# One pool of buffers for rounded and float tiles, and a fourth operand buffer for weights, in a two-layer fp32 trunk

## The chip, the cores and the metric

The kernel runs on one core of a Trainium2 chip. The metric is the device time of one execution in microseconds; the lower the better. The core's engines are PE (matrix multiplication; its weight loads are told apart as PEld), DVE (vector), ACT (scalar activations), POOL (general, also called GpSimd) and SP (which here only issues DMA transfers). Each engine works through its own queue of instructions in order, and they wait for each other by semaphores. Data lie in SBUF (128 partitions, about 204 KB of each taken here, which is all that is free); PE writes to eight PSUM tiles of 128 x 512 floats.

## The reference

What is computed is a trunk of two residual layers on x, 1024 tokens of width 1024, with 256 memory tokens, all in float32:

```python
for layer in range(2):
    h = rms_norm(x, norm_mix[layer])
    if layer == 0:      # gated linear recurrence: conv of width 4, two sigmoid gates,
                        # an associative scan over the tokens, a gelu gate
        y_mix, xq = rglru_group(h, w_in_a, ...)
    else:               # 8-head causal attention with a forget gate
        y_mix, xq = fox_group(h, w_in_b, ...)
    y_mem = memory_group(xq, mem, ...)            # 4-head cross-attention into 256 tokens
    x = x + concatenate([y_mix, y_mem], -1) @ w_out[layer]
    x = x + square(relu(rms_norm(x, norm_mlp[layer]) @ w_mlp_in[layer])) @ w_mlp_out[layer]
```

## The kernel before, in words

**Products.** Each float32 operand is split into a rounded high part ("hi", type fp32r) and the rounded rest ("lo"), and a product is the sum of three matrix products: hi x hi, hi x lo, lo x hi (`t3`). So every activation tile needs two rounded buffers, and every weight a high and a low one. `split` and `split_sb` do it for activations: ACT writes hi, DVE subtracts and writes lo. PE accumulates into a PSUM tile, and DVE or ACT reads it out ("evicts" it).

**Buffers.** Activations live in two sets made once at the start: 60 rounded buffers `r` (128 x 512, fp32r) and 23 float buffers `f` (128 x 515, float32; the three more columns are for the convolution's overlap of tokens). `Slots.get` takes the buffer that was given back longest ago, `Slots.put` gives one back. A piece of code that takes a buffer can start when the last reader of the earlier content is done.

**Weights.** `self.plan` lists all weights in the order of use. An SP load brings one into one of two raw buffers `wr` (L241), ACT rounds it into `wh` (L245), DVE or POOL subtracts into `wl` (L246). `wh` and `wl` have three entries each, used in turn; `wnext` hands out entry i after it has issued the split of entry i + 2. Which of a weight's quarters go to POOL is given by `self.pool_parts`, which the program sets anew at each stage and `_wsplit` reads when it issues the split.

**The order.** The program is written with Python generators: a main stage is woven with a side stage at given rates (`weave`). On top of that the framework's scheduler simulates the written program and sets each engine's order by it, so that a buffer that comes free earlier changes the order on several engines.

**Stages.** The tokens are two halves of 512. In the profiled execution, from the span's start: 0 to 150 us the input projections, the memory's keys and values and the first half's recurrence; 150 to 255 us cross-attention (`xattn`) and the second half's projections; 255 to 330 us the first output projection of the first half (`outproj`), with the second half's recurrence (`lru_scan`, `lru_out`) woven in, and that of the second half (`outproj2`); 330 to 1000 us the first MLP; 1000 to 1600 us the attention layer; 1600 to 2206 us the second MLP. An MLP has 8 groups of hidden columns; its second product is done in 4 blocks a group, each with 7 products in place of 8 (a fast matrix product), whose results are added into x tiles that are loaded from and stored to DRAM (`xspill`) for each block.

**Lines that the steps touch.** In `outproj`, each of eight slices is loaded into a float buffer (`load_x`, L400), PE's product is added to it (L790, `f <- f, pspj`) and it is stored (L794). `lru_scan` works on four column blocks in two passes: L744 to L746 on DVE make the scan's factors, then L756, L757 and L758 on DVE: multiply, rescale, scan; `lru_out` multiplies by the gate (L770), and a split follows (L365/L366 or L371/L372: hi on ACT, lo on DVE). L609 is the cross-attention's product with the values, which the split of L371/L372 evicts from PSUM tile `pso`. PSUM tiles are named after their use: `pspj`, `pss`, `pspt`, `pso`. The MLP's products are L923, its first projection and all other projections are issued by L301 (`mmq`).

Of the kernel before, what the change touches and what calls it, by code (L numbers as in the profile page):

```python
# [10 lines left out]
F32 = mybir.dt.float32  # L11
F32R = mybir.dt.float32r
# [7 lines left out]
P = 128  # L20
S = 1024
D = 1024
H = 512
# [27 lines left out]


class Slots:
    def __init__(self, tiles):
        self.free_ = deque(tiles)
        self.low = len(tiles)

    def get(self):
        t = self.free_.popleft()
        self.low = min(self.low, len(self.free_))  # L60
        return t

    def put(self, *ts):
        for t in ts:
            self.free_.append(t)


def drain(g):
# [69 lines left out]


class Builder:  # L140
    NR = 60
    NF = 23
    FW = 515
    PB = {"pj": 2, "s": 2, "pt": 3, "o": 1}

    def __init__(self, ctx, tc, ins, out):
        self.tc, self.nc, self.ins, self.out = tc, tc.nc, ins, out
        nc = self.nc
        cst = ctx.enter_context(tc.tile_pool(name="cst", bufs=1))
        self.sm = ctx.enter_context(tc.tile_pool(name="sm", bufs=2))  # L150
        self.ps = ctx.enter_context(tc.tile_pool(name="ps", bufs=1, space=PSUM))
        self.dr = ctx.enter_context(tc.tile_pool(name="dr", bufs=1, space=DRAM))
        self.cst = cst

        self.R = Slots([cst.tile([P, 512], F32R, name=f"r{i}") for i in range(self.NR)])
        self.F = Slots([cst.tile([P, self.FW], F32, name=f"f{i}") for i in range(self.NF)])
        self.wraw = [cst.tile([P, 1056], F32, name=f"wr{i}") for i in range(2)]
        self.whi = [cst.tile([P, 1056], F32R, name=f"wh{i}") for i in range(3)]
        self.wlo = [cst.tile([P, 1056], F32R, name=f"wl{i}") for i in range(3)]

        self.par = cst.tile([P, NPAR], F32, name="par")
        nc.sync.dma_start(self.par, ins["par"])
        self.ident = cst.tile([P, P], F32, name="ident")
        make_identity(nc, self.ident)
        self.ones = cst.tile([P, P], F32, name="ones")
        nc.vector.memset(self.ones, 1.0)
        self.cD = cst.tile([P, 1], F32, name="cD")
        nc.vector.memset(self.cD, 1.0 / D)
        self.grp = None
        self.grp_prev, self.grp_cur = [], []  # L170
        self.plan = []
        self.ridx, self.nraw = [], 0
        self.wpos = self.wload = self.wrawn = 0
        self.rs_tok = [None, None]
        self.vx = [None, None]
        self.rsb = [None, None]
        self.ss = [None, None]
        self.uid = 0
        self.pool_parts = TUNE["pa"]
        self.done = set()  # L180
        self.zz = {}
        self.xg = [None, None]
        self.ymix = [None, None]
        self.hs = [None, None]
        self.ymem = [None, None]
        self.xqs = [None, None]
# [93 lines left out]
    def wnext(self):  # L280
        i = self.wpos
        self.wpos += 1
        self._wsplit(i + 3)
        return self._wbuf(i, self.whi), self._wbuf(i, self.wlo)

    def wpair(self):
        i = self.wpos
        self.wpos += 2
        self._wsplit(i + 3)
        return [(self._wbuf(j, self.whi), self._wbuf(j, self.wlo)) for j in (i, i + 1)]  # L290


# [391 lines left out]

    def lru_u(self, h, m, ps):
        nc = self.nc
        u = self.F.get()
        nc.vector.tensor_tensor(u[:, 3:515], ps, self.rsb[h][:, :H], ALU.mult)
        nc.vector.tensor_copy(u[:, 0:3], self.halo[m])
        if h == 0:  # L690
            nc.vector.tensor_copy(self.halo[m], u[:, 512:515])
        uc = self.F.get()
        c = uc[:, :H]
        nc.vector.tensor_scalar(c, u[:, 0:512], self.pc("conv", m), self.pc("convb", m), ALU.mult, ALU.add)
        for j in range(1, 4):
            nc.vector.scalar_tensor_tensor(c, u[:, j:j + 512], self.pc("conv", j * 4 + m), c, ALU.mult, ALU.add)
        self.F.put(u)
        return uc

    def lru_gates(self, h, m, uc):  # L700
# [744 lines left out]
def _pack(inp):  # L1445
# [53 lines left out]
    for l in range(2):  # L1499
        put(f"gmix{l}", cols(f["norm_mix"][l]))  # L1500
        put(f"gmem{l}", cols(f["norm_mem"][l]))
        put(f"gmlp{l}", cols(f["norm_mlp"][l]))
        put(f"xq{l}", f["xa_q_gain"][l][:, None])
        put(f"xk{l}", f["xa_k_gain"][l][:, None])
# [29 lines left out]
```

## Time and profile before

| | |
|---|---|
| time, median of 3 runs | 2216.56 us (2213.1 to 2219.6) |
| the profiled execution's own time | 2215.74 us |
| its span in the trace | 2214.1 us |
| mean granted clock of PE | 0.986 of full speed |
| DMA | 307.85 MB, mean 139 GB/s |

The span is the stretch from the first to the last instruction that the trace shows; the execution's own time is 1.6 us longer. The granted clock is the share of full speed that the throttle gave to PE. In a table of stretches each row has the stretch, its length and each engine's busy time with the number of instructions. In a list of waits a row has the waiting engine, the PSUM tile or buffer, the line, what it waited for, and then the total in us, how often, and the longest. In a list of instructions a row has the start in us, the duration in us, engine, line, operation, result <- operands, and in brackets what the wait just before it was for.

### The profile page before, as it was taken

The numbers are of one execution on the slowest core, as the hardware profiler recorded it, in microseconds if no ns is written. First come the engines' busy times: TensorE is split into PE (matmuls) and PEld (weight loads), VectorE is DVE, ScalarE is ACT, GpSimd is POOL, SyncE is SP. The second block draws the span as 40 slices with busy tenths as digits, with TensorE's granted clock in tenths as the row PEclk, the third lists the DMA queues.
The fourth block names the chain that finished last, engine by engine and source line by source line (L and its number), as shares of the span: only waits on it lengthen the run. The fifth ranks groups of instructions, "written<-read, shape, count | busy, mean of one in ns | idle before, by whom it ended". The sixth has DMA issues, their size and how long they took to land. (4 is left out here: it accounts for less than half of the span.)

```text
span 2214.1 us, 31106 instructions
## 1 busy us (share of the span) xinstructions
PE 2138.4 (97%) x10662; PEld 1780.2 (80%) x10662; DVE 1617.9 (73%) x2991; ACT 932.4 (42%) x1852; POOL 983.2 (44%) x952
## 2 busy tenths in 40 slices
PE   7889999999999999998999998999999999999999
PEld 6788777888888888876998997777778888888887
DVE  8997776666666666669677877986787566576667
ACT  5755634222232222334556856765433223232222
POOL 3742421545545545456142452331364454454454
PEclk9989999999999999999999998999999999999999
DMA  5412254435445345345425221364564354354353
GB/s 177 129 58 67 93 178 157 134 123 190 138 129 190 130 136 183 126 134 166 125 87 172 96 73 49 125 193 129 168 209 167 104 187 159 107 190 151 108 194 128
DMA packets 138782, 307.85 MB, mean 139 GB/s; under 512 B 15552, under 2 KB 17664, under 8 KB 138624
## 3 DMA queue, kind: packets, MB, share of 16 engines
q1 hardware_dynamic: 138624, 305.87, 42.9%
q8 instruction: 84, 1.38, 0.3%
q14 instruction: 74, 0.61, 0.1%
HBM read 225.03 MB, written 80.77 MB: 138 GB/s over the span
## 5 line engine op out<-in xcount | busy, mean ns | idle before, releaser
L301 PE MATMUL pspj<-r,wh 128*128 128x512 f32 x2656 | 845.8, 398 | 15.5 <-ACT wh L245 5.6
L301 PEld LDWEIGHTS pspj<-r,wh 128*128 128x128 f32 x2656 | 498.4, 189 | 137.3 <-ACT wh L245 5.6
L301 PE MATMUL pspj<-r,wl 128*128 128x512 f32 x1328 | 528.4, 398 | 0.2 <-DVE wl L246 0.2
L245 ACT ACTIVATE wh<-wr 128x256 fp32r<-128x256 f32 (+3 forms) x497 | 275.3, 581 | 391.1 <-PE pspt L923 194.7
L246 DVE TENSOR_TENSOR wl<-wr,wh 128x256 fp32r<-128x256 f32 (+2 forms) x386 | 303.7, 794 | 67.7 <-ACT wh L245 66.7
L371 ACT ACTIVATE r<-f 128x512 fp32r<-128x512 f32 x250 | 156.8, 631 | 416.7 <-POOL f L881 278.4
L881 POOL TENSOR_TENSOR f<-f 128x512 f32<-128x512 f32 x128 | 167.6, 1310 | 320.0 <-DVE f L880 317.3
L301 PEld LDWEIGHTS pspj<-r,wl 128*128 128x128 f32 x1328 | 251.2, 189 | 60.9 <-DVE wl L246 0.7
L301 PE MATMUL pspj<-wh,r 128*128 128x256 f32 (+1 forms) x1408 | 275.5, 290 | 15.2 <-ACT f L450 5.1
L372 DVE TENSOR_TENSOR r<-f,r 128x512 fp32r<-128x512 f32 x250 | 190.3, 773 | 132.8 <-ACT r L371 132.6
L923 PE MATMUL pspt<-r,wh 128*128 128x512 f32 x768 | 246.8, 395 | 1.2 <-ACT f L948 1.0
L301 PEld LDWEIGHTS pspj<-wh,r 128*128 128x128 f32 x1408 | 225.9, 193 | 19.8 <-ACT f L450 6.0
L301 PE MATMUL pspj<-wl,r 128*128 128x256 f32 (+1 forms) x704 | 201.8, 288 | 5.0 <-DVE wl L246 5.0
L960 POOL TENSOR_TENSOR f<-f,f 128x512 f32<-128x512 f32 x64 | 96.3, 1505 | 230.8 <-DVE f L959 218.5
L923 PEld LDWEIGHTS pspt<-r,wh 128*128 128x128 f32 x768 | 144.1, 188 | 36.5 <-ACT wh L245 1.4
L923 PE MATMUL pss<-r,wh 128*128 128x512 f32 x512 | 161.6, 396 | 3.5 <-DVE f L968 3.5
L923 PE MATMUL pspj<-r,wh 128*128 128x512 f32 x512 | 161.2, 396 | 1.4 <-DVE f L949 1.2
L923 PE MATMUL pspt<-r,wl 128*128 128x512 f32 x384 | 152.4, 397 | 0.9 <-DVE wl L246 0.9
L246 POOL TENSOR_TENSOR wl<-wr,wh 128x256 fp32r<-128x256 f32 (+2 forms) x111 | 89.7, 831 | 132.5 <-ACT wh L245 129.0
L301 PEld LDWEIGHTS pspj<-wl,r 128*128 128x128 f32 x704 | 135.5, 193 | 6.7 <-DVE wl L246 5.8
L245 ACT ACTIVATE wh<-f 128x512 fp32r<-128x512 f32 x128 | 80.4, 630 | 143.2 <-PE pspj L923 61.3
L880 DVE SCALAR_TENSOR_TENSOR f<-pspj,f 128x512 f32<-128x512 f32 x128 | 87.7, 687 | 66.4 <-PE pspj L301 66.1
(273 smaller groups left out, 3635.5 us busy)
## 6 DMA issues: line engine op xcount, KB each, us to landing
f<-xspill SPq DMA_DIRECT2D x312, 256.0 KB, 3.0
xspill<-f SPq DMA_DIRECT2D x288, 256.0 KB, 3.0
wr<-in_w_dram SPq DMA_DIRECT2D x134, 512.0 KB, 4.1
f<-in_xT_dram SPq DMA_DIRECT2D x32, 256.0 KB, 3.7
wr<-in_wkv_dram SPq DMA_DIRECT2D x16, 512.0 KB, 3.9
wr<-in_wina_dram SPq DMA_DIRECT2D x15, 512.0 KB, 3.8
f<-cscr SPq DMA_DIRECT2D x24, 256.0 KB, 3.5
wr<-in_wxqa_dram SPq DMA_DIRECT2D x8, 512.0 KB, 3.8
```

The source lines that it names most:

```text
L245: self.nc.scalar.activation(hi, raw, AF.Copy)
L246: eng.tensor_tensor(lo, raw, hi.bitcast(F32), ALU.subtract)
L301: self.nc.tensor.matmul(out, lhsT=a, rhs=b, start=(j == 0), stop=(j == n - 1))
L371: self.nc.scalar.activation(hi[:, :n], src, AF.Copy)
L372: self.nc.vector.tensor_tensor(lo[:, :n], src, hi[:, :n].bitcast(F32), ALU.subtract)
L880: nc.vector.scalar_tensor_tensor(r[:, n], ps, 0.0, self.rsb[h][:, n], ALU.max, ALU.mult)
L881: nc.gpsimd.tensor_tensor(r[:, n], r[:, n], r[:, n], ALU.mult)
L923: nc.tensor.matmul(ps, lhsT=a, rhs=b, start=(j == 0), stop=(j == 5))
L960: G.tensor_tensor(c12, c12, u, ALU.add)
```

## The change

The two sets of persistent buffers go. In their place stands one deque of 77 indices, from which both `Slots` take: `get` makes a new tile of 128 x 512, of the type asked for, under the tag of the index, with one buffer for each tag, so that a rounded tile may come to lie where a float tile was. Buffers are still taken in the order in which they were given back, but now out of one queue. The convolution's input, the only user of the three more columns, gets two buffers of its own, `ubuf`, used in turn. The rings `wh` and `wl` have four entries in place of three, and `wnext` issues the split of entry i + 3. SBUF is as full as before: 204,052 bytes a partition before, 204,056 now.

```diff
 class Slots:
-    def __init__(self, tiles):
-        self.free_ = deque(tiles)
+    def __init__(self, pool, dtype, free, held):
+        self.pool, self.dtype, self.free_, self.held = pool, dtype, free, held

     def get(self):
-        t = self.free_.popleft()
+        i = self.free_.popleft()
+        k = len(self.held)
+        t = self.pool.tile([P, H], self.dtype, tag=f"u{i}", bufs=1, name=f"{'f' if self.dtype == F32 else 'r'}{i}_{k}")
+        self.held.append(t)
+        t_ids[id(t)] = i
         return t

     def put(self, *ts):
         for t in ts:
-            self.free_.append(t)
+            self.free_.append(t_ids.pop(id(t)))
...
 class Builder:
-    NR = 60
-    NF = 23
-    FW = 515
+    NU = 77
+    NRING = 4
...
-        self.R = Slots([cst.tile([P, 512], F32R, name=f"r{i}") for i in range(self.NR)])
-        self.F = Slots([cst.tile([P, self.FW], F32, name=f"f{i}") for i in range(self.NF)])
+        up = ctx.enter_context(tc.tile_pool(name="up", bufs=1))
+        free, held = deque(range(self.NU)), []
+        self.R = Slots(up, F32R, free, held)
+        self.F = Slots(up, F32, free, held)
+        self.ubuf = [cst.tile([P, H + 3], F32, name=f"ub{i}") for i in range(2)]
...
-        self.whi = [cst.tile([P, 1056], F32R, name=f"wh{i}") for i in range(3)]
-        self.wlo = [cst.tile([P, 1056], F32R, name=f"wl{i}") for i in range(3)]
+        self.whi = [cst.tile([P, 1056], F32R, name=f"wh{i}") for i in range(self.NRING)]
+        self.wlo = [cst.tile([P, 1056], F32R, name=f"wl{i}") for i in range(self.NRING)]
...
     def wnext(self):
-        self._wsplit(i + 3)
+        self._wsplit(i + self.NRING)
...
     def lru_u(self, h, m, ps):
-        u = self.F.get()
+        u = self.ubuf[m % 2]
...
-        self.F.put(u)
```

What the scheduler makes of it is seen in the engines' orders. The first pair is DVE's, in the first output projection. In the names `f_138`, `r_119` and the like the number tells tiles apart; `hsl` is the state handed on from the first half's scan, `par` a parameter. Before (L756 to L758 are the scan's steps, L790 adds a PSUM tile to x, L770 is the gate, L366 and L246 write low parts):

```order
L756 TENSOR_TENSOR f_138<-f_138,f_137 128x512
L757 TENSOR_SCALAR f_133<-f_133 128x512
L758 SCALAR_TENSOR_TENSOR f_126<-f_134,hsl_200,f_132 128x512
L366 SCALAR_TENSOR_TENSOR r_119<-f_128,par,r_118 128x512
L756 TENSOR_TENSOR f_148<-f_148,f_129 128x512
L757 TENSOR_SCALAR f_136<-f_136 128x512
L246 TENSOR_TENSOR wl_155<-wr_149,wh_152 128x512
L758 SCALAR_TENSOR_TENSOR f_137<-f_133,hsl_201,f_138 128x512
L770 SCALAR_TENSOR_TENSOR f_130<-f_130,f_126 128x512
L790 TENSOR_TENSOR f_142<-f_142,pspj_2774 128x512
L758 SCALAR_TENSOR_TENSOR f_129<-f_136,hsl_202,f_148 128x512
```

In the changed program, where these lines stand seven or eight higher (L763 to L765, L777, L797, L254):

```order
L763 TENSOR_TENSOR f_229_2303<-f_229_2303,f_228_2302 128x512
L764 TENSOR_SCALAR f_284_2819<-f_284_2819 128x512
L380 TENSOR_TENSOR r_273_2759<-pspt_2753,r_272_2758 128x512
L765 SCALAR_TENSOR_TENSOR f_224_2285<-f_283_2817,hsl_150,f_225_2286 128x512
L777 SCALAR_TENSOR_TENSOR f_241_2433<-f_241_2433,f_220_2268 128x512
L797 TENSOR_TENSOR f_287_2842<-f_287_2842,pspj_2847 128x512
L254 TENSOR_TENSOR wl_79<-wr_71,wh_75 128x1024
L765 SCALAR_TENSOR_TENSOR f_228_2302<-f_284_2819,hsl_151,f_229_2303 128x512
```

The last of the four scans (`hsl_202` before, `hsl_151` now) stood right ahead of the seventh addition and stands now ahead of the fourth; three slices' additions that came ahead of it now come after it.

The second pair is SP's queue, at the start of the same stage. Before (L400 loads a slice of x, L241 a weight, L794 stores a slice):

```order
L400 DMA f_145<-in_xT_dram 128x512
L241 DMA wr_149<-in_wout_dram 128x1024
L794 DMA xspill<-f_145 128x512
L241 DMA wr_150<-in_wout_dram 128x1024
L400 DMA f_142<-in_xT_dram 128x512
L794 DMA xspill<-f_142 128x512
```

And in the changed program (L408, L249, L801):

```order
L408 DMA f_287_2842<-in_xT_dram 128x512
L408 DMA f_292_2899<-in_xT_dram 128x512
L408 DMA f_359_3448<-in_xT_dram 128x512
L249 DMA wr_72<-in_wout_dram 128x1024
L249 DMA wr_71<-in_wout_dram 128x1024
L408 DMA f_276_2770<-in_xT_dram 128x512
L408 DMA f_266_2697<-in_xT_dram 128x512
```

Three loads of x, which belong to later slices, stand ahead of two weight loads; those of the first two slices, f_276 and f_266, come behind them.

More of the change, by code (lines that the diff above doesn't have):

```diff
@@ L53 @@
 class Slots:
-    def __init__(self, tiles):
-        self.free_ = deque(tiles)
-        self.low = len(tiles)
+    def __init__(self, pool, dtype, free, held):
+        self.pool, self.dtype, self.free_, self.held = pool, dtype, free, held
     def get(self):
-        t = self.free_.popleft()
-        self.low = min(self.low, len(self.free_))
+        i = self.free_.popleft()
[3 more added lines that the diff above has]
+        t_ids[id(t)] = i
         return t
@@ L64, in put @@
         for t in ts:
-            self.free_.append(t)
+            self.free_.append(t_ids.pop(id(t)))
+t_ids = {}
 def drain(g):
@@ L288, in wpair @@
         self.wpos += 2
-        self._wsplit(i + 3)
+        self._wsplit(i + self.NRING)
         return [(self._wbuf(j, self.whi), self._wbuf(j, self.wlo)) for j in (i, i + 1)]
```

## The prediction

> **What bounds the kernel now.** I read the page's first part, then the busy time cut into the kernel's stages, then the waits and the timeline of the stages where TensorE is not full.
>
> ```profile
> span 2214.1 us, 31106 instructions
> PE 2138.4 (97%) x10662; PEld 1780.2 (80%) x10662; DVE 1617.9 (73%) x2991; ACT 932.4 (42%) x1852; POOL 983.2 (44%) x952
> PE 31%; DMA 1%; DVE 1%; ACT 1%; issue 0%; POOL 0%; POOLq 0%; SPq 0%; DVEq 0%; ACTq 0%
> ```
>
> PE, the matmul engine, is busy for 2138.4 of 2214.1 us, so all its idle time together is 75.7 us. The chain that ended last goes through PE, and the instructions that only wait ("issue", "DVEq", "ACTq") hold 0% of it: what a few more of them cost, I put at nothing.
>
> ```profile
> core 0: us, PE busy (x) PEld busy (x) DVE busy (x) ACT busy (x) POOL busy (x), PEclk, DMA share, GB/s
> 0.00:150.00 150.00, 124.02 (x706) 107.39 (x707) 138.83 (x286) 91.88 (x192) 75.72 (x73) 0.92 0.40 127
> 150.00:255.00 105.00, 105.00 (x605) 91.18 (x605) 77.93 (x155) 64.80 (x143) 38.31 (x48) 1.00 0.24 73
> 255.00:330.00 75.00, 66.27 (x272) 52.07 (x271) 56.98 (x83) 32.54 (x53) 24.62 (x17) 0.93 0.49 158
> 330.00:1000.00 670.00, 669.05 (x2873) 538.26 (x2872) 449.80 (x668) 206.97 (x328) 312.27 (x274) 1.00 0.46 148
> 1000.00:1070.00 70.00, 57.96 (x327) 49.80 (x326) 65.34 (x150) 36.16 (x84) 34.09 (x26) 0.93 0.54 171
> 1200.00:1230.00 30.00, 25.26 (x154) 20.94 (x153) 25.12 (x63) 22.33 (x55) 10.00 (x14) 1.00 0.65 210
> 1300.00:1510.00 210.00, 192.44 (x1143) 163.24 (x1142) 170.86 (x456) 134.56 (x324) 77.50 (x109) 0.97 0.38 118
> 1600.00:2206.00 606.00, 605.35 (x2600) 487.94 (x2599) 421.50 (x618) 180.20 (x285) 309.55 (x268) 1.00 0.47 155
> ```
>
> Each row is a stretch: PE, weight loads, DVE, ACT, POOL, granted clock. The two MLPs (330 to 1000, 1600 to 2206) have PE full to 1.6 us in 1276: nothing can be won there, only lost. What can be won lies elsewhere, as idle PE and as clock: 150 - 124.0 = 26.0 us and 0.08 x 150 = 12 us in the first stage; 8.7 and 0.07 x 75 = 5.3 us from 255 to 330; 12.0 and 4.9 us around 1035; 4.7 us at 1215; 17.6 and 6.3 us in the attention stage. In the first stage and around 1035 DVE is the limit (138.8 of 150, 65.3 of 70), and the change takes no work from DVE. The stage that I argue from is 255 to 330, where the first output projection runs beside the second half's scan.
>
> ```profile
> PE pso L609 <- DVE r L372: 3.4, 1, 3.4
> PE pspj L301 <- ACT r L371: 3.2, 1, 3.2
> PE pspt L818 <- ACT wh L245: 1.5, 1, 1.5
> PE pspj L301 <- DVE f L790: 0.6, 1, 0.6
> SPq L400 <- DVE f L758: 8.4, 4, 5.2
> 269.03 1.89 DVE L745 SCALAR_TENSOR_TENSOR f<-f,f 128x512 f32<-128x512 f32 x3
> 271.44 0.68 DVE L372 TENSOR_TENSOR r<-pso,r 128x512 fp32r<-128x512 f32 x1
> 297.49 0.70 PE L301 MATMUL pspj<-r,wh 128*128 128x512 f32 x2 [3.17 <-ACT r L371]
> 294.90 1.27 DVE L758 TENSOR_TENSOR_SCAN f<-f,hsl,f 128x512 f32<-128x512 f32 x1
> 296.67 0.67 DVE L790 TENSOR_TENSOR f<-f,pspj 128x512 f32<-128x512 f32 x1
> ```
>
> The first five rows are waits (total, times, longest). PE waits 3.4 us for an eviction (L372) that stands on DVE behind three scan steps (L745), and 3.2 us until 297.49; the page names ACT, but L790, which empties the PSUM tile, ends at 297.34, and it stood behind the scan (L758). And x loads (L400) wait 8.4 us for float buffers that the scan holds: 23 are too few here.
>
> **The change, part by part.**
>
> *One pool of 77 for 60 + 23.* No arithmetic is added or removed. Buffers go round in the order in which they are given back, so what counts is how far back in program order the next free one was given back. I counted that by walking the program, in PSUM tiles written in between. Before, float buffers at the projections and at the scan come back after 0 to 3 tiles with as few as 1 spare; with the pool after 3 to 6 with 3 or more spare. So the scan is freed, and the scheduler places it earlier. The two orders of DVE shown with the change are from the first output projection (the changed program's lines are some seven higher: L758 is L765 there, L790 L797). The last scan stands behind the third of eight additions; before, behind the sixth. What moved ahead, at most: four L745, four L746, three L744, three L756 and L757, two L758.
>
> ```profile
> L756 DVE TENSOR_TENSOR f<-f,f 128x512 f32<-128x512 f32 x4 | 6.0, 1499 | 0.0
> L758 DVE TENSOR_TENSOR_SCAN f<-f,hsl,f 128x512 f32<-128x512 f32 x4 | 5.5, 1383 | 0.0
> L746 DVE TENSOR_SCALAR f<-f 128x512 f32<-128x512 f32 x4 | 3.2, 832 | 0.0
> L757 DVE TENSOR_SCALAR f<-f 128x512 f32<-128x512 f32 x4 | 2.7, 683 | 0.0
> L745 DVE SCALAR_TENSOR_TENSOR f<-f,f 128x512 f32<-128x512 f32 x4 | 2.6, 688 | 2.3 <-POOL f L360 2.3
> L744 DVE TENSOR_SCALAR f<-f 128x512 f32<-128x512 f32 x2 | 0.8, 419 | 0.0
> ```
>
> That is 4 x 0.688 + 4 x 0.832 + 3 x 0.419 + 3 x 1.499 + 3 x 0.683 + 2 x 1.383 = 16.7 us of DVE, out of a stretch where PE waits for DVE and into 150 to 255, where DVE idles 105 - 77.9 = 27.1 us and PE never does. At stake is 8.7 + 5.3 = 14.0 us. But PE now needs that work 16.7 us sooner, and if only the last 30 us before it are of use, idle DVE there is 27.1 x 30 / 105 = 7.7 us, which leaves 9.0 us as a new wait; with the clock at 5.3 / 8.7 = 0.6 us for each idle us it costs 14.4 us. Between -14.0 and +14.4 I take -4: the work is ready early (the scan's own L745 waited 2.3 us for a buffer), yet only the two waits named, 6.6 us, are surely the scan's, and one of them may come back earlier.
>
> By the Trainium skill (page "SBUF — State Buffer", section "SBUF: two separate sides") a DVE instruction with two SBUF inputs and a POOL instruction that reads SBUF exclude each other for their whole length. The trace agrees: L756 takes 1.50 us on average, L745 of the same size 0.69. By that rule the moved steps could stay as long or grow where POOL is busier, which is the slow rival below; POOL is busy 38.3 of 105 us there against 24.6 of 75, the same share within 4%.
>
> *SP's queue at the same place.* Before, one x load (L400) at a time stood among weight loads (L241) and stores (L794); in the second pair of orders, the changed program's, three loads (f_287, f_292, f_359) stand ahead of two weight loads and of two more loads of x. The three are later slices; the first two slices (f_266, f_276) come last, because their buffers are those of the cross-attention just ending. Queued behind the three are the two weight loads, and PE waits for those. This is part of the +14.4 bound, not a new term.
>
> *The fourth operand buffer.* ACT and DVE split the next weight one entry sooner. In the MLP that buys nothing, since PE waits for no weight there:
>
> ```profile
> ACT wh L245 <- PE pspt L923: 108.1, 56, 5.1
> PE pspt L301 <- DVE wl L246: 4.6, 1, 4.6
> PE pspj L301 <- DVE wl L246: 5.2, 4, 2.7
> ```
>
> The split waits for PE (108.1 us in the first MLP), not PE for it. PE's waits for weights, 9.8 us, are in the first stage, and there DVE has 150 - 138.8 = 11.2 us of idle time: the bound is -9.8. Walking the waits, PE at the end of that stage needs as many DVE instructions as before, so I take 0, and +5 as the other end (half the 11.2 us lost).
>
> *Pool for DVE.* Which engine subtracts is read when the split is issued, now one weight sooner: DVE gets four quarter subtractions and gives up one half.
>
> ```profile
> 88.33 0.42 DVE L246 TENSOR_TENSOR wl<-wr,wh 128x256 fp32r<-128x256 f32 x1
> 294.30 0.68 DVE L246 TENSOR_TENSOR wl<-wr,wh 128x512 fp32r<-128x512 f32 x1
> ```
>
> That is 4 x 0.42 - 0.68 = +1.0 us, counted in full, as DVE is the limit early on. The two buffers for the convolution input (ubuf) cost nothing: they alternate, as two of the 23 did, and DVE alone touches them.
>
> *Loads for the second attention half (1200 to 1230).*
>
> ```profile
> PE pspj L301 <- ACT r L365: 2.1, 2, 1.8
> ```
>
> PE waits for a split (L365) of x tiles that are loaded into float buffers; by the walk those are now given back 17 tiles before, instead of 9. I take -2 of the 4.7 us; ends -4.7 and 0. For the attention stage (1300 to 1510) the walk finds reuse a little shorter in some places and longer in others: 0, with ends -6 and +6, a quarter of its 23.9 us.
>
> *The MLPs.* Here float buffers come back after 4 to 6 products, before 9 or more. One product is 1.40 us, a load or store lands after 3.0 us:
>
> ```profile
> 1609.23 1.40 PE pspj L923 x6
> f<-xspill SPq DMA_DIRECT2D x312, 256.0 KB, 3.0
> xspill<-f SPq DMA_DIRECT2D x288, 256.0 KB, 3.0
> ```
>
> A tile stored at product 6 of a block is loaded anew from product 4 of the next (5 products, 7.0 us, against 0.7 + 3.0 us for the add and the store) and first needed four to seven products later (at least 5.6 us, against 3.0 us): 2 to 3 us to spare each time. I take 0; if the cover goes, next late is the addition that empties PSUM.
>
> **The sum.** -4 + 0 + 1 - 2 + 0 + 0 = -5 us. The profiled execution took 2215.74 us, 0.8 below the median of 2216.56. So 2215.7 - 5 = 2211 us, 0.25% below the median. A difference under 0.3% (6.6 us, that is 2209.9 to 2223.2) cannot be told from none here, so this is "no change" on its faster side.
>
> **The rivals.**
> - *All three places gain in full.* For it: x loads wait on the scan's buffers, PE on evictions behind the scan. Against: PE needs the scan sooner. Time: 2215.7 - 14.0 - 4.7 + 1 = 2198, with part of the first stage 2192; say 2200.
> - *Nothing moves.* DVE stays the limit wherever PE waits, and each wait gone at 269 comes back at another tile. Time 2216.
> - *Slower: PE waits at the head of the first output projection.* Place: 240 to 265 us, where PE is full now. The first two x tiles load late and their additions stand behind the scan. Price +14.4, with the -2 and +1 left: 2215.7 + 13 = 2229. It is slower than the bound once over 6.6 + 1.8 us, that is about 5 us of wait with its clock.
> - *Slower: the MLPs lose the reuse distance.* 64 blocks (2 layers x 8 groups x 4); at 0.25 us each 16 us, 2227. It decides from (2223.2 - 2210.7) / 64 = 0.2 us a block. Against it: 2 to 3 us to spare.
>
> By the Trainium skill (page "TensorE: Matmul & The Clock Gate", section "What's actually happening") the clock is halved after an idle window of about 3.4 us and restored after a busy one. The trace agrees: the clock is 1.00 where PE has no gaps and 0.93 where it has waits of 3.4 and 3.2 us. By that rule alone, taking away both long waits gives the whole 5.3 us of clock beside 6.6 us, and the stage would gain 11.9 us: the time of the first rival.
>
> **The numbers.** Forecast (2207 to 2215): 0.40, of it 0.10 below 2209.9. Full gain: 0.26. Nothing: 0.12. Slow head of the projection: 0.14. MLP: 0.08. Faster 0.10 + 0.26 = 0.36; same 0.30 + 0.12 = 0.42; slower 0.14 + 0.08 = 0.22. The range goes from 2193, short of the full gain with the first stage, to 2229, the slow ends, and leaves out about 0.15; the forecast's own is 2207 to 2215.
>
> **What would show it.** Right: the wait of L609 for an eviction gone, scan steps before 265 us, the clock above 0.95 from 255 to 330, PE still full in both MLPs. Wrong: a PE wait for L797 or a weight between 240 and 265 us; idle PE at the products (L923's line) in the MLPs; the first stage longer or shorter than 150 us by over 5 us, which my equal count of DVE work rules out.

## The result, and the profile after

The changed kernel took 2236.79 us (median of 4 runs, 2234.7 to 2238.9) against 2218.08 us before: a ratio of 1.0088, with a 95% interval of 1.0075 to 1.0101. It is slower by 18.7 us. A second time, on another chip, the ratio was 1.0109 (1.0092 to 1.0126). The forecast was 2211 us, with a range from 2193 to 2229 us; the measured time lies above it.

The page of the changed kernel begins like this (span; busy time of each engine), and the row below gives span and granted clock:

```profile
span 2233.0 us, 31336 instructions
PE 2147.5 (96%) x10662; PEld 1784.7 (80%) x10662; DVE 1645.3 (74%) x2994; ACT 927.9 (42%) x1852; POOL 989.7 (44%) x949
core 0: 2233.0 us, clock 0.984
```

PE is idle for 2233.0 - 2147.5 = 85.5 us, 9.8 more than before, and busy for 9.1 more with the same 10662 products. At a mean clock of 0.984 the throttle took 0.016 x 2233.0 = 35.7 us, before 0.014 x 2214.1 = 31.0: some 5 more, as an estimate, since a step of 0.001 in the clock is 2.2 us, and since PE is idle in a part of the halved time. Another part of the longer busy time shows in the stretch from 1700 to 2200 us, where PE is full in both kernels. Before, and then after (stretch, length, then busy time and count of PE, weight loads, DVE, ACT, POOL, clock, DMA):

```profile
1700.00:2200.00 500.00, 500.00 (x2148) 403.20 (x2148) 338.50 (x497) 146.54 (x231) 249.74 (x217) 1.00 0.46 151
```

```profile
1700.00:2200.00 500.00, 500.00 (x2142) 401.76 (x2142) 345.64 (x491) 144.54 (x228) 254.52 (x218) 1.00 0.47 155
```

In the same 500 us at full clock PE issues 6 products fewer: one every 233.4 ns, before every 232.8. The kernel has 7260 products of 512 columns (the sum of their counts over all lines); at 0.6 ns each that is 4.4 us. So the 18.9 us of the span are 9.8 us of idle PE and 9.1 us of longer busy time, of which slower products are some 4.4 us. In the halved stretches PE is busy for 53.5 us before and 58.0 after, which makes 2.2 us of the rest; the last 2.5 us are not assigned.

Where it was lost shows when the two executions are compared at the same count of PE products done:

| products done | 500 | 750 | 1250 | 1750 | 4250 | 6000 | 7750 | 8500 | 10660 |
|---|---|---|---|---|---|---|---|---|---|
| time before, us | 111.1 | 155.5 | 244.1 | 369.1 | 952.7 | 1238.7 | 1531.0 | 1706.3 | 2209.5 |
| after, us later | 6.7 | 2.5 | 10.2 | 6.7 | 8.3 | 8.1 | 13.5 | 16.6 | 19.0 |

It loses 2.5 us in the first stage, 7.7 in the cross-attention, wins 3.5 in the output projections, loses 1.6 in the first MLP, 5.4 in the attention stage and 5.5 in the last stretch. The table of stretches, after:

```profile
0.00:150.00 150.00, 121.76 (x694) 105.65 (x695) 137.45 (x279) 91.82 (x195) 79.78 (x75) 0.93 0.39 126
150.00:255.00 105.00, 99.46 (x561) 85.68 (x560) 81.09 (x159) 61.11 (x132) 37.74 (x43) 0.96 0.24 77
255.00:330.00 75.00, 69.04 (x302) 56.14 (x301) 54.21 (x84) 33.87 (x61) 21.21 (x21) 0.93 0.45 146
330.00:1000.00 670.00, 669.22 (x2867) 537.55 (x2866) 458.09 (x661) 204.96 (x325) 313.14 (x272) 1.00 0.47 150
1300.00:1510.00 210.00, 190.72 (x1149) 162.06 (x1149) 169.01 (x454) 132.56 (x327) 79.72 (x110) 0.96 0.33 100
```

From 150 to 255 us PE was full before at clock 1.00; now it is idle for 5.5 us and the clock is 0.96. The waits of PE from 230 to 330 us (engine, tile, line, waited for; total, times, longest), after:

```profile
PE pspj L309 <- DVE f L797: 6.0, 1, 6.0
PE pss L304 <- ACT f L217: 3.0, 2, 2.8
PE pspt L627 <- DVE xnb L592: 2.5, 1, 2.5
```

The two waits of before (L609 for an eviction, 3.4 us; L301, 3.2 us) are gone, and three others of 11.5 us stand in their place. The lists of instructions show why (rows of PE, ACT, POOL and DVE in the changed kernel, by start; in brackets the wait just before):

```profile
244.80 0.42 DVE L753 TENSOR_SCALAR f<-f 128x512 f32<-128x512 f32 x1
245.14 2.34 DVE L752 SCALAR_TENSOR_TENSOR f<-f,f 128x512 f32<-128x512 f32 x2
247.41 0.15 DVE L592 TENSOR_SCALAR xnb<-xnb 128x2 f32<-128x2 f32 x1
...
247.66 0.47 ACT L217 ACTIVATE f<-pss,xnb 128x256 f32<-128x256 f32 x1 [2.79 <-DVE xnb L592]
...
248.73 1.65 PE L304 MATMUL pss<-r,r 128*128 128x256 f32 x6 [2.83 <-ACT f L217]
...
265.73 5.62 POOL L762 TENSOR_TENSOR f<-f,f 128x512 f32<-128x512 f32 x4 [1.78 <-ACT f L217]
...
267.06 1.76 DVE L763 TENSOR_TENSOR f<-f,f 128x512 f32<-128x512 f32 x1 [2.58 <-POOL f L762]
268.75 1.48 DVE L764 TENSOR_SCALAR f<-f 128x512 f32<-128x512 f32 x1
270.26 2.17 DVE L765 TENSOR_TENSOR_SCAN f<-f,hsl,f 128x512 f32<-128x512 f32 x1
272.35 0.66 DVE L763 TENSOR_TENSOR f<-f,f 128x512 f32<-128x512 f32 x1
272.93 0.41 DVE L764 TENSOR_SCALAR f<-f 128x512 f32<-128x512 f32 x1
273.27 0.67 DVE L797 TENSOR_TENSOR f<-f,pspj 128x512 f32<-128x512 f32 x1
...
274.00 1.22 PE L309 MATMUL pspj<-r,wh 128*128 128x512 f32 x2 [5.96 <-DVE f L797]
```

At 245 us the scan's first pass (L752) stands on DVE ahead of a step of the softmax that takes 0.15 us (L592); ACT's exponential waits for that and PE for ACT. At 267 us DVE itself waits for POOL with the scan at the head of its queue, and the first addition (L797), for which PE waits 6.0 us, stands behind five scan steps. While POOL's L762 runs (265.73 to 271.35) the steps L763 and L764 take 1.76 and 1.48 us, right after it 0.66 and 0.41: a part of the wait, 2.2 us, is this lengthening.

### The profile page after: what moved, and what is told of

It is laid out like the page before. It is cut to its first block, busy times and chain, and to the rows that moved or that the text cites. A ratio compares the mean times of both kernels' runs of the same rounds, so it can differ in the third digit from the quotient of the medians.

```text
span 2233.0 us, 31336 instructions
## 1 busy us (share of the span) xinstructions
PE 2147.5 (96%) x10662; PEld 1784.7 (80%) x10662; DVE 1645.3 (74%) x2994; ACT 927.9 (42%) x1852; POOL 989.7 (44%) x949
## 5 line engine op out<-in xcount | busy, mean ns | idle before, releaser
L254 DVE TENSOR_TENSOR wl<-wr,wh 128x256 fp32r<-128x256 f32 (+3 forms) x389 | 305.9, 794 | 43.1 <-ACT wh L253 41.4
L888 POOL TENSOR_TENSOR f<-f 128x512 f32<-128x512 f32 x128 | 153.4, 1198 | 373.2 <-DVE f L887 365.4
L380 DVE TENSOR_TENSOR r<-f,r 128x512 fp32r<-128x512 f32 x250 | 189.7, 772 | 79.3 <-ACT r L379 75.4
L967 POOL TENSOR_TENSOR f<-f,f 128x512 f32<-128x512 f32 x64 | 119.0, 1859 | 190.5 <-DVE f L966 122.5
L887 DVE SCALAR_TENSOR_TENSOR f<-pspj,f 128x512 f32<-128x512 f32 x128 | 87.8, 687 | 94.2 <-PE pspj L309 93.5
L254 DVE TENSOR_TENSOR wl<-f,wh 128x512 fp32r<-128x512 f32 x128 | 114.4, 895 | 51.0 <-ACT wh L253 50.8
L254 POOL TENSOR_TENSOR wl<-wr,wh 128x256 fp32r<-128x256 f32 (+2 forms) x108 | 90.3, 859 | 137.0 <-ACT wh L253 128.9
```

What stands on the lines that cost most here:

```text
L254: eng.tensor_tensor(lo, raw, hi.bitcast(F32), ALU.subtract)
L380: self.nc.vector.tensor_tensor(lo[:, :n], src, hi[:, :n].bitcast(F32), ALU.subtract)
L887: nc.vector.scalar_tensor_tensor(r[:, n], ps, 0.0, self.rsb[h][:, n], ALU.max, ALU.mult)
L888: nc.gpsimd.tensor_tensor(r[:, n], r[:, n], r[:, n], ALU.mult)
L967: G.tensor_tensor(c12, c12, u, ALU.add)
```

## The experiments

All ratios are to the kernel before, run on the same chip, with 95% intervals. "Idle" is span less PE's busy time and "distance" the mean distance between the starts of back-to-back products of 512 columns, both from the profiled execution; the distance is good to 0.1 ns. The row "changed" is the run after_again, the changed kernel on another chip than at first.

| kernel | buffers | apart, bytes | ring | us | ratio | idle, us | distance, ns |
|---|---|---|---|---|---|---|---|
| before | 60 r + 23 f | 2048, f 2080 | 3 | 2216.6 | 1 | 75.7 | 232.7 |
| split_tiles | 60 + 23, new tiles | 2048, f 2080, mixed | 3 | 2208.2 | 0.9981 (0.9973-0.9990) | 74.5 | 232.2 |
| scan_R | 60 + 23, new tiles | mixed | 3 | 2210.1 | 0.9984 (0.9975-0.9993) | 73.2 | 232.4 |
| split_F22 | 60 + 22, new tiles | mixed | 3 | 2211.9 | 0.9993 (0.9984-1.0002) | 77.9 | 232.6 |
| c82 | one queue, 82 | 2080 | 3 | 2209.7 | 0.9980 (0.9971-0.9989) | 80.1 | 232.0 |
| c78 | one queue, 78 | 2080 | 4 | 2211.6 | 0.9991 (0.9983-1.0000) | 80.7 | 231.7 |
| c76 | one queue, 76 | 2080 | 4 | 2219.1 | 1.0021 (1.0012-1.0029) | 82.9 | 232.2 |
| c76u | 76 + 2 set apart | 2080 | 4 | 2219.6 | 1.0024 (1.0014-1.0034) | 79.3 | 232.1 |
| nu76 | 76 + 2 | 2048 | 4 | 2227.8 | 1.0068 (1.0054-1.0081) | 80.0 | 233.4 |
| pads | 77 + 2 | 2048, gaps | 4 | 2228.7 | 1.0066 (1.0052-1.0080) | 85.6 | 232.0 |
| changed | 77 + 2 | 2048 | 4 | 2238.7 | 1.0109 (1.0092-1.0126) | 83.9 | 233.4 |
| look3 | 77 + 2 | 2048 | 4, old lead | 2230.1 | 1.0076 (1.0064-1.0089) | 83.1 | 233.4 |
| ring3 | 77 + 2 | 2048 | 3 | 2231.2 | 1.0076 (1.0062-1.0089) | 86.2 | 232.7 |
| ring3_75 | 75 + 2 | 2048 | 3 | 2231.8 | 1.0079 (1.0064-1.0095) | 85.8 | 232.6 |
| ring3_81 | 81 + 2 | 2048 | 3 | 2216.6 | 1.0016 (1.0007-1.0025) | 82.1 | 232.7 |

**Which part of the change?** The first theory was the order that comes from the common queue (A); rivals were the fourth ring entry (B) and the new tile for each get (C). The ring alone taken back:

```diff
-    NRING = 4
+    NRING = 3
```

> One pool of 77 as in the changed kernel, ring of three weight entries as before. Theory A (the common queue costs, by the orders that the scheduler makes from it): 2230 to 2238 us, about 0.8% over before. Theory B (the fourth ring entry costs: weights are split one entry sooner and stand ahead of evictions on ACT and DVE): 2212 to 2220 us, no difference from before. Theory C (a new tile for every get costs, by more waits: 910 wait instructions on DVE before, 1048 after): 2230 to 2238, as A.

Measured: 2231.19 us, 1.0076. The ring kept, and only the lead taken back:

```diff
-        self._wsplit(i + self.NRING)
+        self._wsplit(i + 3)
```

> The changed kernel with four ring entries, but the split issued only three entries ahead. Theory A: 2230 to 2238 us, as the changed kernel. Theory B: 2212 to 2222 us. Theory C: 2230 to 2238 us. If this and the ring of three differ from each other by over 3 us, it is the reuse of the ring's entries and not the lead that counts.

Measured: 2230.13 us, 1.0076 (1.0064 to 1.0089). Neither ring nor lead carries most of the loss; B falls. What the fourth entry does all the same is told with the fourth operand buffer below. Two sets as before, but a new tile for each get:

```diff
+        t = self.pool.tile([P, self.w], self.dtype, tag=f"{self.pre}{i}", bufs=1, ...)
...
+        self.R = Slots(up, F32R, self.NR, 512, "r")
+        self.F = Slots(up, F32, self.NF, self.FW, "f")
```

> The kernel before with its two sets of 60 and 23 and its ring of three, but each get makes a new tile under the tag of its buffer, as the changed kernel does. Same buffers in the same succession as before. Theories A and B: 2213 to 2221 us, no difference from before. Theory C: 2230 to 2238 us.

Measured: 2208.18 us, 0.9981: C falls, it is even a little faster, though the engines' orders are not quite those of before (at 219 of DVE's 2991 places stands another instruction). What is left is the queue, or something that came with it.

**The one place with the late loads.**

```diff
-    NU = 77
+    NU = 75
...
+            if res and m < 2:
+                x = self.xres[m]
+                nc.sync.dma_start(x, src[m, :, h * H:(h + 1) * H])
```

> The changed kernel with a pool of 75 and two buffers of their own for the x tiles of the first two slices of the first output projection (in the changed kernel these load late, into buffers of the cross-attention, and the scan stands ahead of their additions on DVE). Theory A, in the form that late loads bring about this wait: the wait of 6.0 us for L797 at 268 us goes, with about 3 us of halved clock: 2226 to 2230 us. Theory A in a form without a single place (the order is worse everywhere), B and C: 2234 to 2239 us, the idle time comes back nearby.

Measured: 2231.89 us, 1.0084, between the two forecasts. PE's waits from 230 to 330 us in that kernel:

```profile
PE pso L618 <- DVE r L381: 8.9, 3, 7.4
PE pspj L310 <- DVE xres L803: 1.8, 1, 1.8
PE pspt L628 <- POOL f L602: 1.0, 1, 1.0
```

The wait of 6.0 us is gone, and one of 7.4 us for an eviction that now stands behind the scan has come: the idle time moved.

**The freed scan by itself.** Two sets, and only the second half's scan takes its r0 and t from the larger one:

```diff
+        B = self.R if h else self.F
...
-            r0 = self.F.get()
+            r0 = B.get(F32)
...
-            t = self.F.get()
+            t = B.get(F32)
```

> The kernel with two sets, ring of three and a new tile for each get (2208.2 us), but in the second half's scan alone the five float tiles that it takes (r0 of each column block and t) come from the set of 60, which has spare ones there. It frees the scan as the common queue does, and touches nothing else; by the order, PE then needs 5 to 12 us more of DVE work between 240 and 270 us. Theory A1 (what costs is the freedom: side work that was held back by short float buffers is put ahead of work that PE needs): 2212 to 2218 us, with idle PE at the cross-attention's scores around 245 to 255 us or at the first additions. Rival A2 (what costs in the common queue is buffers that come back late, across types; freeing the scan is a gain): 2198 to 2208 us, PE's waits at 269 and 294 us gone.

Measured: 2210.08 us, 0.9984, against 0.9981 without it: nothing that the intervals could show, and both theories had a difference. PE's waits from 230 to 330 us in it:

```profile
PE pspj L309 <- DVE f L800: 5.8, 1, 5.8
PE pss L304 <- ACT f L217: 1.6, 1, 1.6
```

The waits of 3.4 and 3.2 us went, as forecast, and 5.8 us for the first addition and 1.6 us at the scores came: 6.6 for 7.4. This is the step of my prediction in pure form, and it is worth zero within some 2 us.

**How many buffers?** Room of the ring's fourth entry given to the queue:

```diff
-    NRING = 4
-    NU = 77
+    NRING = 3
+    NU = 81
```

> One pool, ring of three, and 81 buffers in place of 77, in the room of the fourth ring entry. Theory A1: 2228 to 2235 us, as with 77 (2231.2): buffers are not what anything waits for. Rival A2: faster by a part of the loss, 2217 to 2226 us, since each buffer comes back four gets later.

Measured: 2216.62 us, 1.0016, 14.6 us less than with 77. A1 fell here and with scan_R. Two queues that borrow, with the ring of four and then of three:

```diff
+        i = (self.free_ if self.free_ else self.other.free_).popleft()
...
+        self.R = Slots(up, F32R, deque(range(56)), held)
+        self.F = Slots(up, F32, deque(range(56, self.NU)), held)
```

> The changed kernel (77 tiles, ring of four, convolution buffers of their own), but with two queues, 56 indices for rounded and 21 for float tiles, and a get takes from the other queue only when its own is empty. Theory A1: floats are short again and hold the side work back: by the order PE needs 2 to 5 us more of DVE work than before from 1200 to 1450 matrix products and 11 to 17 us less at 550 to 700; 2205 to 2220 us. Theory A2: also 2205 to 2220 us, as the types don't mix. If it stays at 2230 or more, it is neither the order of the queue nor the freedom of the floats.

Measured: 2238.12 us, 1.0105 (1.0090 to 1.0120).

> The same two queues with borrowing, ring of three, 60 and 21 indices. It differs from the kernel with two sets and new tiles (2208.2 us) by the convolution buffers and the borrowing alone. Both theories: 2203 to 2213 us. Against the one above it shows the ring of four by itself: if the fourth entry is worth nothing, the two are within 5 us.

Measured: 2225.53 us, 1.0050 (1.0037 to 1.0062). With the types kept apart but for borrowing, the loss stayed, in full with the ring of four and 0.5% with the ring of three, where both theories had none: mixing them isn't the cause by itself. The two are 12 us apart and not within 5, so the fourth entry is not shown to be worth nothing; they also differ by four indices. The next theory was that only the count of buffers matters (N).

```diff
-    NU = 77
-        self.ubuf = [cst.tile([P, H + 3], F32, name=f"ub{i}") for i in range(2)]
-        u = self.ubuf[m % 2]
+    NU = 82
+    FW = 515
+        u = self.F.get()
```

> One queue, ring of three, and nothing set apart: 82 buffers of 515 columns, of which the convolution takes its own as before. Against the two sets with new tiles (83 buffers, 2208.2 us) only the queue is common, and one buffer is missing. Theory N (what counts is how many buffers go round: four more were worth 14.6 us, 3.6 us each): 2209 to 2214 us. Rival M (81 with two set apart stayed 8.4 us above the two sets because a common queue has a price of its own): 2214 to 2220 us.

Measured: 2209.65 us, 0.9980: as fast as the two sets. M falls. The same with `NU = 78` and the ring of four:

> The changed kernel (one queue, ring of four) with the convolution's two buffers given back to the queue: 78 of 515 columns in place of 77 of 512 and two set apart. Theory N: one buffer more goes round, about 3.6 us less than the changed kernel: 2226 to 2231 us. Rival (the two set apart cost nothing, one buffer is within the noise): 2231 to 2236 us.

Measured: 2211.58 us, 0.9991. Both expectations were wrong by 14 us or more: one buffer more, and the whole loss was gone. `NU = 75` in ring3, and 22 floats in split_tiles:

> One queue, ring of three, 75 buffers in place of 77 (2231.2 us) and 81 (2216.6 us). Theory N: about 7 us more, 2235 to 2242 us. Rival S (the loss sets in between 81 and 77 at one place and is then spent): 2228 to 2234 us.

Measured: 2231.84 us: no slope from 77 to 75; N falls.

> Two sets with new tiles (2208.2 us), with 22 float buffers in place of 23, so that at the tightest place none is to spare. Theory N: 3 to 4 us more, 2210 to 2214 us. Rival F (floats are what is short in the kernel before, so one less costs far more): 2216 us or more. Rival Z (in two sets a float more or less changes nothing): 2206 to 2210 us.

Measured: 2211.92 us, 0.9993, as N had it, but within 4 us of no change.

**Where the tiles lie.** c78 differs from the changed kernel in three things: one buffer, no convolution buffers set apart, and a tile of 515 columns, so that tiles lie 2080 bytes apart instead of 2048. Its products also came faster (231.7 ns). That led to addresses. The second convolution buffer longer by 13 columns:

```diff
-        self.ubuf = [cst.tile([P, H + 3], F32, ...) for i in range(2)]
+        self.ubuf = [cst.tile([P, H + (3, 16)[i]], F32, ...) for i in range(2)]
```

> The changed kernel with one thing moved: the second convolution buffer is 13 columns longer, so that every buffer behind it, weights and the 77 tiles, lies 32 bytes higher. No instruction and no order on any engine differs. Theory L1 (addresses: in the changed kernel all rounded tiles lie 32 bytes off a multiple of 64, before they lay on one): the matrix products of the MLPs come every 232.9 ns or less instead of 233.5, some 3 us, and other engines gain as well: 2224 to 2231 us. Theory U (the two convolution buffers taken out of the round cost) and theory L2 (the pitch counts, not the offset): 2231 to 2236 us, as the changed kernel.

Measured: 2237.85 us, 1.0104 (1.0084 to 1.0124): L1 falls, an offset alone does nothing. 76 wide tiles with the convolution buffers, and then without:

> The changed kernel with its two convolution buffers, with 76 tiles of 515 columns (2080 bytes apart) in place of 77 of 512 (2048 bytes apart). Theory L2 (the pitch of 2048 bytes costs, since all tiles then start at the same place of a 2048-byte row): near the kernel with 78 such tiles and no convolution buffers, 2211.6: 2210 to 2218 us. Theories U and L1: 2231 to 2238 us.

Measured: 2219.56 us, 1.0024: 1.6 us above L2's range and far below that of U and L1.

> The same 76 tiles of 515 columns, and the convolution takes its buffers from them, as in the kernel with 78. Theory U: 2211 to 2216 us here, and 20 us more in the run with the two convolution buffers. Theories L1 and L2: within 4 us of that run.

Measured: 2219.11 us, 1.0021. The two convolution buffers cost nothing; U falls. The control:

> The changed kernel itself, on the same chip as the three others. All theories: 2230 to 2237 us.

Measured: 2238.65 us, 1.0109. Now 76 tiles at 2048 bytes: on all engines the instructions, their order and their waits are those of c76u, and only addresses differ.

```diff
-    NU = 77
+    NU = 76
```

> The changed kernel with 76 tiles in place of 77, of 512 columns, 2048 bytes apart. Every engine's instructions, their order and their waits are the same as in the kernel with 76 tiles of 515 columns and convolution buffers (2219.6 us); only the addresses of the tiles differ. Theory L2 (the pitch): 2232 to 2242 us. Theory W (the count of tiles and the order that comes of it: 76 happens to give a better order than 77): 2217 to 2223 us.

Measured: 2227.75 us, 1.0068, between the two theories. In ratio it is 0.44% over c76u, which is 9.7 us, and the intervals are apart. From 1700 to 2200 us, nu76 and then c76u:

```profile
1700.00:2200.00 500.00, 499.71 (x2139) 401.02 (x2138) 351.86 (x491) 145.86 (x230) 253.51 (x216) 1.00 0.47 155
```

```profile
1700.00:2200.00 500.00, 499.67 (x2151) 403.74 (x2150) 357.84 (x497) 146.14 (x231) 259.31 (x217) 1.00 0.47 154
```

PE is full in both, and does 12 products more with the wider pitch: 499.71 / 2139 = 233.6 ns against 232.3. 1.3 ns on 7260 products are 9.4 us, which is the whole difference. Durations on ACT, DVE and POOL agree within 1% in the sum. The last run moved only the addresses of the changed kernel itself:

```diff
+        if i not in seen:
+            seen.add(i)
+            if len(seen) % 3 == 0:
+                self.held.append(self.pool.tile([P, 8], F32, tag=f"gap{i}", bufs=1, ...))
```

> The changed kernel with a gap of 32 bytes behind every third of its 77 tiles, so that they start at 26 different places of a 2048-byte row in place of one. Instructions, orders, waits and the tile that each get takes are the same on every engine. Theory L2 (tiles 2048 bytes apart slow PE's products): products every 232.0 to 232.5 ns in place of 233.5; with 7260 products of 512 columns that is 7 to 10 us, 2227 to 2231 us on a chip where the changed kernel takes 2237. Rival (the width of the tile, or that a product reads a part of a tile, not where it lies): 2235 to 2240 us, products every 233.5 ns.

Measured: 2228.66 us, 1.0066. From 1700 to 2200 us, and the first rows of PE's waits over the whole span:

```profile
1700.00:2200.00 500.00, 499.86 (x2153) 403.65 (x2152) 350.05 (x495) 146.58 (x233) 255.02 (x219) 1.00 0.47 156
PE pspj L314 <- DVE f L802: 7.7, 5, 5.9
PE pspj L314 <- DVE wl L259: 6.9, 2, 5.5
PE pss L309 <- ACT f L222: 6.8, 3, 3.8
```

And the same waits in the changed kernel (its lines are five lower):

```profile
PE pspj L309 <- DVE f L797: 8.3, 5, 6.0
PE pss L304 <- ACT f L217: 7.1, 4, 3.7
PE pspj L309 <- DVE wl L254: 5.7, 2, 5.4
```

The products come as expected (499.86 / 2153 = 232.2 ns), the waits stay where they were, and idle PE is 85.6 us against 85.5. So the loss has two parts, told apart by the same instructions at other addresses. Addresses: the changed kernel loses 5 to 10 us (1.0088 or 1.0109 against 1.0066) against tiles that start at many places of a 2048-byte row. The interval of the first of these ratios overlaps with that of pads; the products say 10 us (1.4 ns on 7260). Order, in the sense of all that is left: at good addresses it is still 0.66%, 14.6 us, slower than before. Against split_tiles, whose products come nearly as fast as those of pads, it is 0.85%, 19 us.

One face of the order's part is idle PE: it was 73 to 78 us in all four kernels with two full sets, and 79 to 89 us in all kernels with a common or a borrowing queue. c82 has that too, 80.1 against 74.5 us of split_tiles; its products come a little faster, and the times agree. Idle PE is not all of it. The mean granted clock of all runs of a kernel on one chip was 0.982 for pads and 0.988 for the kernel before; 0.006 of 2220 us is 13 us, an upper bound, as PE is idle in a part of the halved time. Idle PE gives pads 9.9 us and its faster products take off 5, which leaves some 10 of the 14.6 us to the halved clock: an estimate, but it makes the clock as large a part as the idle time itself. What the count does is not settled: with wide or spread tiles 76, 77 and 78 gave 2219.6, 2228.7 and 2211.6 us. That is no slope. One buffer more or less makes the scheduler write another order, and these orders differ by up to 17 us, some 2 of it from the products' distance (232.0 against 231.7 ns). Which property of an order makes it bad was not found.

## Why the prediction was wrong

- **The freed scan, -4 (from -14.0 to +14.4).** This is the step that failed, in sign. The two waits that I named did go. But the DVE work went in front of the softmax and of the first additions (17 scan steps, 14.4 us, are done ahead of product 1316, where the first addition now stands; before, four steps, 2.1 us, were), and PE waits there: +7.7 us up to product 1250, -3.5 to 1750, together +4.2. The mean of DVE's idle time from 150 to 255 us (27.1 us) said nothing of whether it is idle at the moment when the scan is put there. The slow rival had the mechanism and the wait ("a PE wait for L797"), at 268 to 274 us where it said 240 to 265, and it left out the softmax; its price of 14.4 was three times too high. That POOL is as busy in the one stretch as in the other said as little of the moment: the scan steps ahead of L797 ran beside POOL and were longer for it. scan_R shows the step alone at zero. Of the 24 us between the forecast's -5 and the +19.0 of the trace this step makes 8.2; the rest are the terms below, above all the stretches of the MLPs (7.1), the attention stage (5.4) and the first stage (2.5), all put at 0.
- **"PE at the end of that stage needs as many DVE instructions as before, so I take 0."** It lost 2.5 us there, inside the ends of -9.8 and +5. The lag was 6.7 us at product 500 and was partly won back: a count at the end of a stage misses waits inside it.
- **The fourth operand buffer, 0.** The number nearly came out, 1.0076 with the ring of three or the old lead and 1.0088 to 1.0109 with it, but by luck: two effects cancel that I did not have. PE's waits for `wl` in the first 150 us, in ring3 and then in the changed kernel:

```profile
PE pspj L309 <- DVE wl L254: 11.8, 6, 4.0
PE pss L309 <- DVE wl L254: 3.0, 2, 2.8
PE pss L309 <- DVE wl L254: 2.8, 1, 2.8
PE pspj L309 <- DVE wl L254: 0.3, 1, 0.3
```

  So with the ring of four most of these waits go (before they were 11.0 us, of which I had left out 1.2 at tile `pss`). Other waits come in their place, but at product 750 the changed kernel is 2.5 us behind the kernel before, and ring3 7.1. Against that, products came every 232.6 to 232.8 ns in all five kernels with the ring of three and the rounded tiles 2048 bytes apart (before, ring3, ring3_75, ring3_81, pref3), and every 233.4 to 233.5 ns in all six with the ring of four and that pitch (changed, look3, nu76, res_x, pref, pad32): 0.7 ns on 7260 products, 5 us. The slower products of the result thus came with the fourth entry at this pitch and not with the common queue; which of its addresses does it was not tried.
- **Pool for DVE, +1.** Not seen apart from the rest.
- **Loads at 1200 to 1230 us, -2.** No gain: from product 4250 to 6000 the lag went from 8.3 to 8.1.
- **Attention stage, 0 with ends of 6.** +5.4: the bound was right, the value was not.
- **The MLPs, 0.** The cover held: PE waited for L887 0.8 us in the first and 2.9 us in the second, and the rival of 0.25 us a block did not come. Yet 7.1 us were lost there by the lag (1.6 and 5.5), 3.3 of them to slower products (0.6 ns on some 5450), a term that I did not have.
- **The sum and the range.** The seven stages add up to 19.0 us: 2.5 + 7.7 - 3.5 + 1.6 - 0.2 + 5.4 + 5.5. None left the ends that stood beside it (the MLPs had only the rival of 16 us), but I let each rival come alone, with the others at their middle. The middle of a term whose sign is unknown was taken as 0 where the order was changed everywhere; the runs show that such a change cost idle PE each time it was made in full (79 to 89 us against 73 to 78). With the slow ends of the first and the attention stage, +5 and +6, which I had beside them, the range would have gone to 2229 + 5 + 6 = 2240.
- **The clock.** By the Trainium skill (page "TensorE: Matmul & The Clock Gate", section "What's actually happening") the clock is judged in windows of 3413 ns that run freely. The trace agrees: in the changed kernel the halved stretches last 3.4, 6.8 or 10.2 us (one before 13.7), but for the last, at the span's end; and the one from 248.0 us, 10.2 us long, begins in the wait of 2.83 us from 245.9. It came on top: of the two halved stretches before, 6.8 us from 271.6 and 3.4 us from 298.9, only the second is gone, and the first stands at 271.9 now. So the clock from 255 to 330 us is 0.93 in both kernels, where I had asked for over 0.95, and the 5.3 us that I had hoped to win there were not won.

## What to carry to other kernels

A wait that goes is worth nothing until the trace shows where the work that it held back will stand: look at the queue of the engine that takes it, at that moment, and at whom it delays there. When a change alters what a scheduler sees everywhere, add the slow ends of several stages, not of one. And compare two kernels only with a look at the addresses: a pair with the same instructions costs one run and tells order from layout.

## What was not expected of the hardware

PE's products of 512 columns came every 233.4 to 233.6 ns when all 76 or 77 tiles lay 2048 bytes apart with the ring of four, and every 231.7 to 232.3 ns when they started at 26 or more places of a 2048-byte row. Two pairs show it with the same instructions, at full clock and with PE full: nu76 against c76u, and the changed kernel against pads. By the Trainium skill (page "SBUF — State Buffer", section "SBUF: two separate sides") PE never waits for anyone on SBUF's engine side; nu76 and c76u show that its rate depends on where tiles lie all the same; whether that is a wait for another reader or PE's own two reads was not shown. Shifting all of them by 32 bytes changed nothing. With the ring of three the tiles at 2048 bytes gave 232.7, so the pitch alone does not decide; the fourth entry adds two weight tiles and moves all tiles behind them, and which of the two counts was not tried. The same effect may be why split_tiles was faster than before with the same succession of buffers: 232.2 against 232.7 ns, times 7260, is 4 us of its 5.3; its orders differ in some places too, and that was not tried apart. Which accesses collide was not tested.
